# Additions of squares for the row norms on GpSimd instead of VectorE, in a two-layer hybrid encoder step

## The chip, the cores and the metric

The kernel runs on one core of a Trainium2 chip. The metric is device time in microseconds: 2740.84 us is the median of three runs of the kernel before (2739.1 to 2744.39). Engines are called as in the profile: PE (TensorE), DVE (VectorE), ACT (ScalarE), POOL (GpSimd), SP (the queue that issues most DMAs).

## The reference, cut to what matters

Two layers are computed for 1024 prompt frames and 64 frames of a running stream, 1088 columns in all, in float32. Each layer normalises its input, projects it, mixes it by gated linear attention and differential attention, projects the result (w_out), normalises that and adds it to x, then does the same with a ConvFFN.

```
def rms_norm(x, w):
    y = xf * lax.rsqrt(jnp.mean(xf * xf, axis=-1, keepdims=True) + EPS)
    return y * w
...
    h = rms_norm(x, ln_mix_pre)
    mix = concat([og, od]) @ w_out
    x = x + rms_norm(mix, ln_mix_post)
    h = rms_norm(x, ln_ffn_pre)
    ... ConvFFN ...
    x = x + rms_norm(y @ w_ffn_down, ln_ffn_post)
```

Each `rms_norm` over the 1024 features needs the mean of the squares of a row. The change touches how these squares are summed.

## The kernel before, in words

Features lie on the 128 partitions and in 8 tiles along them; the 1088 frames lie along the free dimension, in three groups (384, 384 and 320 columns, `GROUPS`). A float32 matmul is made of three passes over high and low halves of the operands (XH/XL, WH/WL, MH/ML), each with a float32r type. So every weight block costs one ACT copy (line 290, WH) and one DVE subtraction (line 269 by way of line 129, WL), and every activation that is multiplied again costs the same.

The order of each engine's instructions is written by the Python program itself, in one pass (manual schedule). `fm_block` emits a block of 24 matmuls (8 feature tiles by 3 passes) and puts off its eviction by one block. Between blocks `pump` emits steps of generators that wait in three queues: `front` (norm sums, entered with `soon` and a due time), `side` (the chains below) and `idle`. What decides is a modelled clock: `clock["pe"]` grows with every matmul and `clock["dve"]` with every call through the wrapper `V` (class `Vector`, lines 118 to 131, so that every DVE instruction carries line 129). A `front` entry is due at the greater of the PE clock plus 1.0 and the DVE clock plus 0.5; a `side` step is emitted only while the DVE clock is less than 1.5 us ahead of the PE clock. A call of `nc.gpsimd` leaves both clocks alone. Each engine then executes its own list strictly in that order.

Two stages hold the norms that the change touches.

- **Stage C** (once in each layer): w_out times the mixer output, 8 blocks a group. `ev_wo` has ACT copy each block to ACC (line 1238) and square it (line 1225 for the first, 1229 after it, into one of the two buffers `EX` in TMP). `sq_flush` (line 1218) adds that square to SQ. Then come, for the group g, `acc_norm`: `ssum` (three matmuls of 384 or 320 columns of SQ with ONE, a sum over partitions), `rstd` (ACT line 436, POOL line 437), one block later `bcast` (three matmuls with IDN, ACT copies the result to RB, line 446). After it `chain(which=1)` takes 8 steps, one for each feature tile k: ACC times RB (DVE), times a weight plus the old x in XH (DVE), square by ACT into one of the two buffers `sqb` (line 499), and the addition of the square before it to SQ (line 498, the last at 503). After the eighth, `x_norm` does `ssum`, `rstd` and `bcast` again, and eight more steps make the new XH and XL (DVE, ACT line 514, DVE). The up projection of the group waits for these.
- **Stage D** (end of each layer): the down projection, 8 blocks a group. `ev_dn` adds the block to ACC (DVE), ACT squares it, `sq_flush` adds it to SQ. In the first layer `acc_norm`, `chain(which=3)` and `x_norm` follow: each of 8 steps has three DVE operations (times RB; times weight plus XH; the XL part in `tail`), two on ACT (lines 527, 528) and one addition to SQ (line 484). In the second layer only the first sum is needed, for the outputs.

`ssum` stands in PE's list, and PE takes its list in order: as long as SQ isn't complete, all matmuls behind `ssum` wait. There are 21 such sums: six in each stage C, six in the first layer's stage D, three in the second layer's. In the texts below S means such a sum of squares, B the broadcast one block behind it; acc 0 to 2 are those of `acc_norm` for the groups 0 to 2, x 0 to 2 those of `x_norm`.

POOL's list holds before the change the `pow` of line 437, the small operations of the attention's row norm (lines 1166 to 1168, 831), and DMAs: x to the DRAM buffer XS (lines 501, 533), ConvFFN values to YD (line 1296), queries and keys to QSd and KSd (line 914).

Of the kernel before, what the change touches and what calls it, by code (L numbers as in the profile page):

```python
# [14 lines left out]
ALU = mybir.AluOpType  # L15
# [36 lines left out]
def hybrid_kernel(ctx: ExitStack, tc: tile.TileContext,  # L52
# [6 lines left out]
    nc = tc.nc  # L59
# [71 lines left out]
    V = Vector()  # L131

    def f(ap):
        return ap.bitcast(F32)
# [55 lines left out]
    def soon(gen, key, more=0.0):  # L190

        front.append([gen, max(clock["pe"] + 1.0, clock["dve"] + 0.5) + more, key])
# [185 lines left out]
    def ln(l, i, k):  # L378
        return VC[:, l, 264 + i * 8 + k:265 + i * 8 + k]
# [49 lines left out]
    def ssum(g, b):  # L429

        for j in range(3):
            t0 = tt(3 * g + j)
            mm(PS[:, b, j:j + 1], SQ[:, t0:t0 + 128], ONE, start=True, stop=True)

    def rstd(g, b, dst):
        act(dst, PS[:, b, 0:3], AF.Identity, scale=1.0 / D, bias=EPC)
        nc.gpsimd.tensor_tensor(dst, dst, NEGH[:, 0:3], ALU.pow)

    def bcast(g, b, src):

        for j in range(3):
            mm(PS[:, b, j * 128:(j + 1) * 128], src[:, j:j + 1].to_broadcast([128, 128]), IDN,
               start=True, stop=True)
        t0, n = GROUPS[g]
        if g < 2:
            act(RB[:, t0:t0 + n], PS[:, b, :n], AF.Copy)
        else:
            act(RB[:, t0:t0 + 256], PS[:, b, :256], AF.Copy)
            act(RB[:, SEQ:T], PS[:, b, 320:384], AF.Copy)
# [16 lines left out]
    def chain(l, g, which, tag):  # L466

        t0, n = GROUPS[g]
        sqb = TMP[:, 2316:3084].rearrange("p (r t) -> p r t", r=2)
        nl, nw = (l, 2) if which == 1 else (l + 1, 0)  # L470
        rb = RB[:, t0:t0 + n]
        sq = SQ[:, t0:t0 + n]
        while ("acc", g) not in done:
            yield "acc", g
        done.remove(("acc", g))

        def a(k):
            return accv[:, k, t0:t0 + n]

        def tail(k):  # L480
            V.scalar_tensor_tensor(XL[:, k, t0:t0 + n], a(k), ln(nl, nw, k),
                                   f(XH[:, k, t0:t0 + n]), ALU.mult, ALU.subtract)
            if k:
                V.tensor_tensor(sq, sq, sqb[:, k % 2, :n], ALU.add)
        def x_norm():
            ssum(g, 5)
            rstd(g, 5, RS[:, 3 * g:3 * g + 3])
            yield 1.6
            bcast(g, 6, RS[:, 3 * g:3 * g + 3])
            done.add((tag, "rs", g))  # L490
            yield

        if which == 1:
            for k in range(8):
                V.tensor_tensor(a(k), a(k), rb, ALU.mult)
                V.scalar_tensor_tensor(a(k), a(k), ln(l, which, k), f(XH[:, k, t0:t0 + n]), ALU.mult, ALU.add)
                if k > 1:
                    V.tensor_tensor(sq, sq, sqb[:, (k - 1) % 2, :n], ALU.add)
                act(sqb[:, k % 2, :n] if k else sq, a(k), AF.Square)
                if k % 4 == 3:  # L500
                    nc.gpsimd.dma_start(XS[:, k - 3:k + 1, t0:t0 + n], accv[:, k - 3:k + 1, t0:t0 + n])
                if k == 7:
                    V.tensor_tensor(sq, sq, sqb[:, 1, :n], ALU.add)
                    soon(x_norm(), (tag, "rs", g))
                yield
            while (tag, "rs", g) not in done:
                yield tag, "rs", g

            def low(k):
                x = XH[:, k, t0:t0 + n]  # L510
                V.tensor_tensor(XL[:, k, t0:t0 + n], a(k), f(x), ALU.subtract)
            for k in range(8):
                V.scalar_tensor_tensor(a(k), a(k), ln(nl, nw, k), rb, ALU.mult, ALU.mult)
                act(XH[:, k, t0:t0 + n], a(k), AF.Copy)
                if k:
                    low(k - 1)
                if k == 7:
                    low(7)
                    done.add((tag, "x", g))
                yield  # L520
            return
        V.tensor_tensor(a(0), a(0), rb, ALU.mult)
        for k in range(8):
            if k < 7:
                V.tensor_tensor(a(k + 1), a(k + 1), rb, ALU.mult)
            V.scalar_tensor_tensor(a(k), a(k), ln(l, which, k), f(XH[:, k, t0:t0 + n]), ALU.mult, ALU.add)
            act(XH[:, k, t0:t0 + n], a(k), AF.Copy, scale=ln(nl, nw, k))
            act(sqb[:, k % 2, :n] if k else sq, a(k), AF.Square)
            if k:
                tail(k - 1)  # L530
            if k == 7:
                tail(7)
                nc.gpsimd.dma_start(XS[:, :, t0:t0 + n], accv[:, :, t0:t0 + n])
                done.add((tag, "x", g))
                soon(x_norm(), (tag, "rs", g), 3.0 if which == 3 else 0.0)
            yield
# [677 lines left out]
    def sq_flush():  # L1214

        if st.get("sq"):
            sq, j = st.pop("sq")
            V.tensor_tensor(sq, sq, j, ALU.add)

    def sq_add(src, g, first):  # L1220

        t0, n = GROUPS[g]
        sq = SQ[:, t0:t0 + n]
        if first:
            act(sq, src, AF.Square)
        else:
            st["sqi"] = st.get("sqi", 0) + 1
            j = EX[:, st["sqi"] % 2, :n]
            act(j, src, AF.Square)
        sq_flush()  # L1230
        if not first:
            st["sq"] = (sq, j)

    def ev_wo(m, g, first, last):
        t0, n = GROUPS[g]

        def ev(b):
            act(accv[:, m, t0:t0 + n], PS[:, b, :n], AF.Copy)
            sq_add(PS[:, b, :n], g, first)
            if last:  # L1240
                sq_flush()
        return ev
# [263 lines left out]
    def ev_dn(first, last, m, g):  # L1506
        t0, n = GROUPS[g]

        def ev(b):
            a = accv[:, m, t0:t0 + n]  # L1510
            if first:
                act(a, PS[:, b, :n], AF.Copy)
            else:
                V.tensor_tensor(a, PS[:, b, :n], a, ALU.add)
            if last:
                sq_add(a, g, m == 0)
                if m == 7:
                    sq_flush()
                if l + 1 == DEPTH:
                    act(a, a, AF.Copy, scale=ln(l, 3, m))  # L1520
        return ev
# [59 lines left out]
    for l in range(DEPTH):  # L1581
# [168 lines left out]
        def c_blocks():  # L1750
            ring["banks"] = (0, 1, 2, 3, 4, 7)
            for g in range(3):
                residual(g)
            for n, (g, i, w) in enumerate(plan):
                m, u = L["wo"][i]
                if w:
                    want(wo[0] + w)
                fm_block(u, g, wo_rhs, ev_wo(m, g, n % 8 == 0, n % 8 == 7))
                yield
                pump(3)  # L1760
                if n % 8 == 7:
                    flush()
                    soon(acc_norm(g), ("acc", g))
                    beside(chain(l, g, 1, tag))
# [44 lines left out]
        for p in range(NP):  # L1809
            n, i = divmod(p, 7)  # L1810
# [70 lines left out]
        n = L["dn", 18]  # L1881
# [3 lines left out]
        for g in range(3):  # L1885
            ahead = range(6) if g == 0 else ()
            bs = {m: bank() for m in ahead}
            for m in ahead:
                dn_mms(bs[m], (18, 19), m, g, True, False)
                pump()  # L1890
            for m in range(8):
                if m in bs:
                    b = bs[m]
                    dn_mms(b, (20, 21), m, g, False, True)
                else:
                    b = bank()
                    dn_mms(b, (18, 19, 20, 21), m, g, True, True)
                if l + 1 < DEPTH and g == 2 and m == 6:
                    want_part(768)
                defer(lambda m=m, g=g, b=b: ev_dn(False, True, m, g)(b))  # L1900
                pump()
            if g == 2:
                want(n + 5)
            flush()
            if l + 1 < DEPTH:
                soon(acc_norm(g), ("acc", g))
                beside(chain(l, g, 3, ("D", l)))
            else:
                if g < 2:
                    soon(out_norm(g), ("acc", g))  # L1910
                else:
                    drain()
                beside(outputs(g))
# [31 lines left out]
```

## Time and profile before

| What | Value |
|---|---|
| median of 3 runs | 2740.84 us (2739.1 to 2744.39) |
| profiled execution | 2747.34 us, its span 2745.6 us |
| mean granted TensorE clock | 0.991 |
| PE busy | 2685.3 us |
| DVE busy | 1783.5 us, 3632 instructions |
| ACT busy | 1205.2 us |
| POOL busy | 271.9 us, 453 instructions |
| additions of squares on DVE | 98 of 128x384 (54.3 us) and 49 of 128x320 (23.8 us) |
| stage C of the first and the second layer | about 525 to 645 us and 1881 to 2000 us of the span |
| stage D with its norms | about 1327 to 1440 us and 2682 to 2745 us |

The profile comes from one execution. A row of a timeline gives the start, the length, engine, line, operation, output and inputs with their shapes, how many instructions were merged, and in brackets the idle time of the engine before it with what ended it. Starts of DVE operations that follow each other lie a little closer than their lengths, because they overlap by some 0.08 us.

### The profile page before, as it was taken

Reading aid. Unit: us, or ns where it says so; the run is one execution under the profiler, and the core shown is the slowest. Engines: PE = TensorE matmul, PEld = TensorE weight load, DVE = VectorE, ACT = ScalarE, POOL = GpSimd, SP = SyncE. Lnnn points to the kernel's source line nnn. Section 1 sums busy time; section 2 is a strip of 40 time slices with the busy share of each in tenths; the row PEclk is TensorE's granted clock in tenths of the full one; section 3 lists DMA queues with packets and bytes.
Section 4 is the critical chain, followed back from the end, with each engine's and each line's share of the span. In section 5 each row is a group of like instructions: output and inputs, shape, how many; then the busy total and the mean of one; then the engine's idle time right before and its main releaser. Section 6 shows DMA issues by size and latency. Waiting matters only on the chain.

```text
span 2745.6 us, 48446 instructions
## 1 busy us (share of the span) xinstructions
PE 2685.3 (98%) x19271; PEld 2626.4 (96%) x19271; DVE 1783.5 (65%) x3632; ACT 1205.2 (44%) x2484; POOL 271.9 (10%) x453
## 2 busy tenths in 40 slices
PE   8999999999999999999999999999899999999999
PEld 8999989999999999999999999889899999999998
DVE  5443458577898888445772334684788988883455
ACT  5333348555533434412343343684554333443125
POOL 2200024201000000000021000341010000000000
PEclk9999999999999999999999999999999999999999
DMA  7421176432222222323452213744331222233233
GB/s 251 142 72 51 56 194 150 127 108 80 65 87 80 71 74 94 112 85 98 136 188 86 64 42 85 206 107 134 117 95 51 78 88 71 71 108 104 73 122 124
DMA packets 296938, 284.62 MB, mean 104 GB/s; under 512 B 15438, under 2 KB 264680, under 8 KB 296712
## 3 DMA queue, kind: packets, MB, share of 16 engines
q1 hardware_dynamic: 272584, 214.14, 27.0%
q0 software_dynamic: 17344, 63.58, 6.3%
q10 hardware_dynamic: 6784, 3.81, 0.5%
q8 instruction: 152, 2.49, 0.4%
q14 instruction: 74, 0.61, 0.1%
HBM read 198.85 MB, written 82.62 MB: 103 GB/s over the span
## 4 chain that ended last, share of the span: by engine, by line
PE 85%; DVE 5%; DMA 4%; issue 3%; ACT 2%; POOL 0%; SPq 0%; ACTq 0%; DVEq 0%; POOLq 0%
PE PS L110 82%; PE PS L114 3%; DVE ACC L129 2%; DMA RAW<-in_w_out_dram 1%; DVE SML L129 1%; DMA RAW<-in_w_ffn_up_dram 1%; DVE WL L129 1%; DVE SQ L129 1%; ACT WH L290 1%; DMA out_dram<-TMP 0%; DMA WH<-QSd 0%; DVE ML L129 0%; DMA WH<-KSd 0%; ACT ACC L1112 0%; DVE XL L129 0%
## 5 line engine op out<-in xcount | busy, mean ns | idle before, releaser
L110 PE MATMUL PS<-XH,WL 128*128 128x272 f32 (+2 forms) x3600 | 664.3, 303 | 0.0
L110 PEld LDWEIGHTS PS<-XH,WL 128*128 128x128 f32 x3600 | 541.6, 189 | 0.1
L110 PE MATMUL PS<-XL,WH 128*128 128x384 f32 (+1 forms) x1680 | 399.2, 331 | 0.0
L110 PE MATMUL PS<-MH,WL 128*128 128x272 f32 (+2 forms) x1872 | 387.0, 304 | 0.0
L110 PE MATMUL PS<-XH,WH 128*128 128x384 f32 (+1 forms) x1296 | 322.0, 333 | 4.9 <-DVE TMP L129 2.7
L110 PEld LDWEIGHTS PS<-XL,WH 128*128 128x128 f32 x1680 | 299.2, 191 | 0.0
L110 PEld LDWEIGHTS PS<-MH,WL 128*128 128x128 f32 x1872 | 289.3, 189 | 0.0
L290 ACT ACTIVATE WH<-RAW 128x1024 fp32r<-128x1024 f32 (+3 forms) x177 | 147.5, 839 | 303.7 <-DMA RAW<-in_w_ffn_down_dram 180.2
L129 DVE TENSOR_TENSOR ACC<-PS,ACC 128x384 f32<-128x384 f32 (+1 forms) x264 | 139.2, 534 | 191.0 <-PE PS L110 190.8
L129 DVE TENSOR_TENSOR WL<-RAW,WH 128x1024 fp32r<-128x1024 f32 (+3 forms) x177 | 167.9, 949 | 114.8 <-ACT WH L290 114.6
L110 PEld LDWEIGHTS PS<-XH,WH 128*128 128x128 f32 x1296 | 229.1, 191 | 6.1 <-DVE TMP L129 3.6
L110 PE MATMUL PS<-XL,WL 128*128 128x272 f32 (+2 forms) x1344 | 230.6, 294 | 0.0
L110 PE MATMUL PS<-MH,WH 128*128 128x384 f32 (+1 forms) x720 | 216.5, 333 | 0.8 <-DVE XL L129 0.8
L110 PE MATMUL PS<-ML,WH 128*128 128x384 f32 (+1 forms) x720 | 214.4, 331 | 1.8 <-DVE ML L129 1.8
L1388 ACT ACTIVATE WL<-ACC 128x512 fp32r<-128x512 f32 x144 | 87.3, 629 | 253.6 <-PE PS L110 161.3
L110 PEld LDWEIGHTS PS<-XL,WL 128*128 128x128 f32 x1344 | 194.7, 188 | 0.0
L129 DVE SCALAR_TENSOR_TENSOR ACC<-ACC,VC 128x1090 f32<-128x1090 f32 x144 | 194.1, 1348 | 0.1
L110 PEld LDWEIGHTS PS<-ML,WH 128*128 128x128 f32 x720 | 134.1, 191 | 2.3 <-DVE ML L129 2.3
L110 PEld LDWEIGHTS PS<-MH,WH 128*128 128x128 f32 x720 | 131.5, 189 | 2.1 <-DVE XL L129 1.1
L129 DVE TENSOR_REDUCE SML<-PS 128x1 f32<-128x384 f32 (+6 forms) x144 | 104.4, 725 | 42.7 <-PE PS L110 41.2
L110 PE MATMUL PS<-WH,XH 128*128 128x256 f32 (+1 forms) x864 | 128.8, 292 | 0.0
L110 PE MATMUL PS<-WH,XL 128*128 128x256 f32 (+1 forms) x864 | 122.8, 285 | 0.0
(255 smaller groups left out, 4725.3 us busy)
## 6 DMA issues: line engine op xcount, KB each, us to landing
RAW<-in_w_ffn_up_dram SPq DMA_DIRECT2D x52, 512.0 KB
RAW<-in_w_in_dram SPq DMA_DIRECT2D x48, 512.0 KB
YD<-ACC POOLq DMA_DIRECT2D x36, 544.0 KB, 3.0
RAW<-in_w_out_dram SPq DMA_DIRECT2D x32, 512.0 KB
XH<-XS SPq DMA_DIRECT2D x8, 1536.0 KB
RAW<-in_w_ffn_down_dram SPq DMA_DIRECT2D x48, 256.0 KB
RB<-YD SPq DMA_DIRECT2D x22, 544.0 KB
SQ<-YD SPq DMA_DIRECT2D x18, 544.0 KB
```

The costliest lines, as they stand in the source:

```text
L110: nc.tensor.matmul(out, lhsT, rhs, **kw)
L114: nc.tensor.transpose(out, in_, idn)
L129: return op(out, *a, **kw)
L290: act(hi, src, AF.Copy)
L1388: act(hi, src, AF.Copy)
```

## The change

The additions of squares at lines 484, 498, 503 and 1218 are issued by `nc.gpsimd` instead of the wrapper `V`. Nothing else in the text changes. There are 147 of them: 84 at line 1218, 42 at 498 and 503, 21 at 484.

```
         def tail(k):
...
             if k:
-                V.tensor_tensor(sq, sq, sqb[:, k % 2, :n], ALU.add)
+                nc.gpsimd.tensor_tensor(sq, sq, sqb[:, k % 2, :n], ALU.add)
...
                 if k > 1:
-                    V.tensor_tensor(sq, sq, sqb[:, (k - 1) % 2, :n], ALU.add)
+                    nc.gpsimd.tensor_tensor(sq, sq, sqb[:, (k - 1) % 2, :n], ALU.add)
                 act(sqb[:, k % 2, :n] if k else sq, a(k), AF.Square)
...
                 if k == 7:
-                    V.tensor_tensor(sq, sq, sqb[:, 1, :n], ALU.add)
+                    nc.gpsimd.tensor_tensor(sq, sq, sqb[:, 1, :n], ALU.add)
                     soon(x_norm(), (tag, "rs", g))
...
             sq, j = st.pop("sq")
-            V.tensor_tensor(sq, sq, j, ALU.add)
+            nc.gpsimd.tensor_tensor(sq, sq, j, ALU.add)
```

Because the additions no longer advance the modelled DVE clock, the program also emits the other instructions in another order. The following piece of the difference is PE's list in stage C of the first layer, ahead of S of x 0 (the row with ONE and SQ); the six rows of a block are one weight block of 24 matmuls.

```order
 L110 MATMUL PS<-MH,WL 128x384 x4
 L110 MATMUL PS<-XL,WL 128x384 x4
-L110 MATMUL PS<-MH,WH 128x384 x4
-L110 MATMUL PS<-XL,WH 128x384 x4
-L110 MATMUL PS<-ML,WH 128x384 x4
-L110 MATMUL PS<-XL,WH 128x384 x4
-L110 MATMUL PS<-MH,WL 128x384 x4
-L110 MATMUL PS<-XL,WL 128x384 x4
 L110 MATMUL PS<-ONE,SQ 128x1 x3
```

S of x 0 stands one block earlier in PE's list. Counted in matmuls behind the B that starts the chain, S of x 0, x 1 and x 2 stood at 96, 120 and 144 before, and all three stand at 72 now, in both layers; the S of acc 1 and acc 2 stand 72 behind the B before them instead of 48 and 24. In stage D of the first layer S of x 0 stands 120 matmuls behind the B of acc 0 instead of 168, S of x 1 147 behind the B of acc 1 instead of 225, and S of x 2 129 behind the B of acc 2 instead of 230.

In the same place POOL's list held these rows before, from the first `pow` of stage C on (SML and RS hold the row scales, XS is x in DRAM).

```order
L437 TENSOR_TENSOR SML<-SML,NEGH 128x3
L501 DMA XS<-ACC 128x4x384 x2
L437 TENSOR_TENSOR RS<-RS,NEGH 128x3
L437 TENSOR_TENSOR SML<-SML,NEGH 128x3
L501 DMA XS<-ACC 128x4x384 x2
```

Now it holds these, from the first additions of stage C to the `pow` of x 0.

```order
L1218 TENSOR_TENSOR SQ<-SQ,TMP 128x384 x7
L437 TENSOR_TENSOR SML<-SML,NEGH 128x3
L498 TENSOR_TENSOR SQ<-SQ,TMP 128x384 x2
L501 DMA XS<-ACC 128x4x384
L498 TENSOR_TENSOR SQ<-SQ,TMP 128x384 x2
L1218 TENSOR_TENSOR SQ<-SQ,TMP 128x384
L498 TENSOR_TENSOR SQ<-SQ,TMP 128x384 x2
L501 DMA XS<-ACC 128x4x384
L503 TENSOR_TENSOR SQ<-SQ,TMP 128x384
L1218 TENSOR_TENSOR SQ<-SQ,TMP 128x384
L437 TENSOR_TENSOR RS<-RS,NEGH 128x3
```

Between the B of acc 0 and S of x 0 POOL has to do seven additions of the chain, one of the next group's blocks ahead of the last, and two DMA issues, all in this order.

In stage D of the first layer POOL's list ends, ahead of the `pow` of x 0, with these rows.

```order
L1218 TENSOR_TENSOR SQ<-SQ,TMP 128x384 x2
L437 TENSOR_TENSOR SML<-SML,NEGH 128x3
L484 TENSOR_TENSOR SQ<-SQ,TMP 128x384 x2
L533 DMA XS<-ACC 1024x1x384
L1218 TENSOR_TENSOR SQ<-SQ,TMP 128x320
L437 TENSOR_TENSOR RS<-RS,NEGH 128x3
```

The last two additions of the chain of group 0 now stand behind the `pow` of acc 1, and so behind S of acc 1 on PE; 14 additions stand between the two `pow` operations of acc 0 and x 0 ahead of the DMA, seven of the chain and seven of the blocks.

More of the change, by code (lines that the diff above doesn't have):

```diff
@@ L483, in tail @@
             if k:
-                V.tensor_tensor(sq, sq, sqb[:, k % 2, :n], ALU.add)
+                nc.gpsimd.tensor_tensor(sq, sq, sqb[:, k % 2, :n], ALU.add)
         def x_norm():
@@ L497, in chain @@
                 if k > 1:
-                    V.tensor_tensor(sq, sq, sqb[:, (k - 1) % 2, :n], ALU.add)
+                    nc.gpsimd.tensor_tensor(sq, sq, sqb[:, (k - 1) % 2, :n], ALU.add)
                 act(sqb[:, k % 2, :n] if k else sq, a(k), AF.Square)
@@ L502, in chain @@
                 if k == 7:
-                    V.tensor_tensor(sq, sq, sqb[:, 1, :n], ALU.add)
+                    nc.gpsimd.tensor_tensor(sq, sq, sqb[:, 1, :n], ALU.add)
                     soon(x_norm(), (tag, "rs", g))
@@ L1217, in sq_flush @@
             sq, j = st.pop("sq")
-            V.tensor_tensor(sq, sq, j, ALU.add)
+            nc.gpsimd.tensor_tensor(sq, sq, j, ALU.add)
     def sq_add(src, g, first):
```

## The prediction

> **What bounds the kernel now.** I read the page's busy times and its chain of work first.
>
> ```profile
> PE 2685.3 (98%) x19271; PEld 2626.4 (96%) x19271; DVE 1783.5 (65%) x3632; ACT 1205.2 (44%) x2484; POOL 271.9 (10%) x453
> PE 85%; DVE 5%; DMA 4%; issue 3%; ACT 2%; POOL 0%; SPq 0%; ACTq 0%; DVEq 0%; POOLq 0%
> ```
>
> PE is the bound. No addition counts as such; what counts is how long PE stands still for SQ. So the waits of PE come next: the whole run, then the windows of the two stages C (515 to 680 and 1870 to 2010 us).
>
> ```profile
> PE PS L110 <- DVE SQ L129: 15.0, 9, 3.0
> ```
> ```profile
> PE PS L110 <- DVE SQ L129: 7.3, 4, 3.0
> ```
> ```profile
> PE PS L110 <- DVE SQ L129: 7.0, 4, 2.5
> ```
>
> SQ is PE's longest wait by far: 15.0 us, of which 7.3 and 7.0 lie in the stages C and 0.7 is left for stage D. These are the prize. Where they stand in the first stage C is in PE's timeline.
>
> ```profile
> 555.75 0.83 PE L110 MATMUL PS<-IDN,SML 128*128 128x128 f32 x6
> 556.34 0.96 PE L110 MATMUL PS<-MH,WH 128*128 128x384 f32 x4
> ...
> 560.61 0.85 PE L110 MATMUL PS<-MH,WH 128*128 128x384 f32 x4
> ...
> 564.77 0.85 PE L110 MATMUL PS<-MH,WH 128*128 128x384 f32 x4
> ...
> 574.73 0.83 PE L110 MATMUL PS<-ONE,SQ 128*128 128x1 f32 x6 [1.47 <-DVE SQ L129]
> 575.42 0.94 PE L110 MATMUL PS<-MH,WH 128*128 128x384 f32 x4
> ...
> 581.24 0.83 PE L110 MATMUL PS<-IDN,RS 128*128 128x128 f32 x6
> ...
> 598.84 0.75 PE L110 MATMUL PS<-MH,WH 128*128 128x320 f32 x4
> ...
> 602.36 0.75 PE L110 MATMUL PS<-MH,WH 128*128 128x320 f32 x4
> ...
> 615.38 0.83 PE L110 MATMUL PS<-ONE,SQ 128*128 128x1 f32 x6 [2.29 <-DVE SQ L129]
> ...
> 627.65 1.15 PE L110 MATMUL PS<-ONE,SQ 128*128 128x1 f32 x6 [2.98 <-DVE SQ L129]
> 628.66 2.91 PE L110 MATMUL PS<-XH,WH 128*128 128x384 f32 x8
> ...
> 635.73 0.83 PE L110 MATMUL PS<-IDN,SML 128*128 128x128 f32 x6
> ```
>
> B of acc 0 is at 555.75; a block of 24 matmuls of 384 columns takes 4.16 us (560.61 to 564.77), of 320 columns 3.52 (598.84 to 602.36). The first block behind a B or S takes 4.27 (556.34 to 560.61). Behind the stop of 1.47 us it takes 5.82 (575.42 to 581.24), 1.6 more, and behind that of 2.98 us 7.07 (628.66 to 635.73), 2.8 more. So a stop costs 1.6 to 2.8 us of slow matmuls on top (2.2 in the mean), though not always.
>
> **What the additions cost on DVE, and what holds the chain of x 0.** ACT and DVE behind that B:
>
> ```profile
> 556.62 0.49 ACT L446 ACTIVATE RB<-PS 128x384 f32<-128x384 f32 x1 [2.97 <-PE PS L110]
> ...
> 559.51 0.52 ACT L499 ACTIVATE TMP<-ACC 128x384 f32<-128x384 f32 x1 [0.60 <-DVE ACC L129]
> ```
> ```profile
> 557.14 0.56 DVE L129 TENSOR_TENSOR ACC<-ACC,RB 128x384 f32<-128x384 f32 x1 [8.72 <-ACT RB L446]
> ...
> 558.27 0.55 DVE L129 TENSOR_TENSOR ACC<-ACC,RB 128x384 f32<-128x384 f32 x1
> ...
> 560.99 1.22 DVE L129 TENSOR_TENSOR WL<-RAW,WH 128x1024 fp32r<-128x1024 f32 x1
> 562.12 0.55 DVE L129 TENSOR_TENSOR ACC<-ACC,RB 128x384 f32<-128x384 f32 x1
> ```
> ```profile
> L129 DVE TENSOR_TENSOR SQ<-SQ,TMP 128x384 f32<-128x384 f32 x98 | 54.3, 554 | 21.7 <-ACT TMP L1229 17.7 <-ACT TMP L499 3.1
> L129 DVE TENSOR_TENSOR SQ<-SQ,TMP 128x320 f32<-128x320 f32 x49 | 23.8, 486 | 1.2 <-ACT TMP L499 0.4 <-ACT TMP L1229 0.2
> ```
>
> DVE loses 78.1 us of busy time. A step of the chain is 1.13 us without its addition (557.14 to 558.27), a WL 1.13. DVE could be through its eight steps, with the two WL among them, 8 x 1.13 + 2 x 1.13 = 11.3 us behind RB. RB is there 1.4 us behind B (555.75 to 557.11), and the first addition can begin 2.9 us behind RB (559.51 + 0.52 = 560.03).
>
> **What they cost on POOL.** The trace has no addition of this size there. What it has are small operations, grouped by tile (least, median and most ns), and one that runs into DVE.
>
> ```profile
> L1166 POOL TENSOR_SCALAR SML<-SML x72: 183/261/1093, 397.2 to 1868.4; 128x1 f32<-128x1 f32 x64, 64x1 f32<-64x1 f32 x8
> ...
> L1168 POOL TENSOR_SCALAR TMP<-TMP,SML x72: 364/372/2101, 398.5 to 1869.3; 128x128 f32<-128x128 f32 x64, 64x128 f32<-64x128 f32 x8
> ...
> L437 POOL TENSOR_TENSOR SML<-SML,NEGH x9: 848/913/1442, 552.0 to 1985.7; 128x3 f32<-128x3 f32 x9
> ```
> ```profile
> 1866.20 2.10 POOL L1168 TENSOR_SCALAR TMP<-TMP,SML 128x128 f32<-128x128 f32 x1
> ```
> ```profile
> 1865.79 2.36 DVE L129 TENSOR_TENSOR WL<-RAW,WH 128x1024 fp32r<-128x1024 f32 x2
> ```
>
> From one to 128 elements an operation with one input tensor grows from 0.18 to 0.36 us, 1.42 ns an element. With one such stream 384 columns take 0.19 + 0.55 = 0.74 us, with two of the same speed 0.19 + 1.09 = 1.28. I take the middle, 1.01 us, of which 0.82 is reading (320 columns: 0.68). [...]
>
> The last two rows matter more. L1168, 0.37 us as a rule, took 2.10 when it fell beside two DVE subtractions with both inputs in SBUF: they end at 1868.15, it ends at 1868.30. POOL could not read while DVE read two tensors. All DVE work of the chain is of that kind (ACC with RB, ACC with XH, RAW with WH). I therefore add the reading time of POOL to the DVE time, whoever of the two waits: an addition that cost DVE 0.47 us from start to start now costs the pair 0.82.
>
> **The sums S of stage C.** The change removes the additions from DVE, and the order shown with the change moves each S of an x to 72 matmuls behind its B.
>
> x 0: PE is at S 3 x 4.16 + 0.6 = 13.1 us behind B. Needed: 1.4 (RB) + 2.9 (before the first addition) + 11.3 - 2.9 = 8.4 (DVE) + 8 x 0.82 = 6.6 (seven additions of the chain, one of a block ahead of the last) = 19.3. Stop 6.2 us, where 1.47 stood.
>
> x 1: PE needs 3 x 3.52 + 0.6 = 11.2; 1.4 + 2.9 + 8.4 + 7 x 0.82 + 0.68 = 19.1. Stop 7.9, where 2.29 stood.
>
> x 2, 320 columns, beside the first blocks of the up projection:
>
> ```profile
> L129 DVE SCALAR_TENSOR_TENSOR ACC<-ACC,VC,XH 128x320 f32<-128x320 f32 x24 | 13.2, 550 | 0.6
> ...
> L129 DVE TENSOR_TENSOR ACC<-ACC,RB 128x320 f32<-128x320 f32 x24 | 11.6, 485 | 0.0
> ```
>
> A step is 0.55 + 0.49 less two overlaps of 0.05, 0.94; eight are 7.5, three weight subtractions 3.4, the convolution of two blocks with three operations of this size 3.2, seven additions 7 x 0.68 = 4.8. With RB 20.3, against 13.1. Stop 7.2, where none stood; what stood there was 144 matmuls away from its B.
>
> acc 1 and acc 2 now have 72 matmuls behind the B of the x before them instead of 48 and 24. Five additions beside the second half of the chain (8 steps of about 1.07) need up to 1.4 + 8.6 + 4.1 = 14.1 against 13.1, and 13.4 against 11.2; since the additions needn't be last, I take 1.5 together, where 0.56 (the 7.3 less the other three waits) and 2.98 stood.
>
> A stage C so stops for 6.2 + 7.9 + 7.2 + 1.5 = 22.8 us instead of 7.3 or 7.0: +31.3 for both. Slow matmuls: three long stops of 2.2 = 6.6 instead of 1.6 + 2.8 = 4.4, +4.4 for both.
>
> **Stage D of the first layer.**
>
> ```profile
> 1340.34 0.83 PE L110 MATMUL PS<-IDN,SML 128*128 128x128 f32 x6
> ```
> ```profile
> 1349.05 0.56 DVE L129 TENSOR_TENSOR ACC<-ACC,RB 128x384 f32<-128x384 f32 x1
> ...
> 1350.58 0.56 DVE L129 TENSOR_TENSOR SQ<-SQ,TMP 128x384 f32<-128x384 f32 x1
> ```
> ```profile
> 1340.00:1365.00 25.00, 21.95 (x137) 21.42 (x137) 23.08 (x48) 13.30 (x27) 1.80 (x2) 1.00 0.00 1
> 1365.00:1380.00 15.00, 12.87 (x78) 12.81 (x77) 11.70 (x25) 7.16 (x15) 1.35 (x2) 0.89 0.42 141
> ```
>
> A chain step is 1.53 us of DVE (1349.05 to 1350.58), eight 12.2. S of x 0 comes 84 matmuls of 384 and 36 of 320 columns behind B, with three S and B between: 14.6 + 5.3 + 1.8 = 21.7 us. Needed: 1.4 + 12.2 + 14 x 0.82 = 25.1: 3.4 us in S of acc 1 and x 0. x 1: 147 matmuls of 320 columns and four S and B, 24.0, against 1.4 + 12.2 + 3.4 (three weight subtractions as at 560.99) + 7 x 0.82 + 7 x 0.68 = 27.5: 3.5. x 2: 129 matmuls of 384, 24.2, against 1.4 + 8 x 1.44 (0.94 and one more operation of 0.50) + 4.8 + 3.4 = 21.1 and what the next layer's first keys and queries put between: I take 1.0, with POOL's DMAs of line 914 among its additions. With two slow stretches of 2.2 that is 12.3. Before, PE was idle for 3.05 and 2.13 us in these two windows (25.00 - 21.95, 15.00 - 12.87), and at a clock of 0.89 lost 1.65 more: 6.8. So +5.5.
>
> **The end of the second layer.**
>
> ```profile
> 2734.24 0.47 ACT L1229 ACTIVATE TMP<-ACC 128x320 f32<-128x320 f32 x1
> ```
> ```profile
> 2736.13 0.73 PE L110 MATMUL PS<-ONE,SQ 128*128 128x1 f32 x6
> ```
>
> The last square is ready 24 matmuls of transposes ahead of this S, at 2734.7; an addition of 1.01 behind it ends by 2735.8. Nothing, 0.4 us if the cover fails.
>
> **The sum.** 31.3 + 4.4 + 5.5 = +41.2 us. The profiled execution took 2747.3 us for a span of 2745.6, 6.5 us above the median of the runs; it becomes 2788.5, and the median 2740.8 + 41.2 = 2782.0, +1.5%. With streams at the fast end (0.55 of reading) each S of an x in C comes 2.2 us earlier and D is 7 us cheaper, 21 us less: 2761. At the slow end it is 21 more: 2803. A measurement of this kernel can tell about 0.2% from no change, 5.5 us.
>
> **The rivals.**
>
> *POOL waits, DVE doesn't.* Then DVE is through at 11.3 us, and each addition is only stretched as L437 was at its longest (1.44 instead of 0.87: 0.57). Up to the end of DVE's steps at 1.4 + 11.3 = 12.7 POOL gets through (12.7 - 4.3) / 1.58 = 5 additions, the other three take 3.0: 15.8, with a DMA issue 16.3. Stops of 3.2, 5.1 and about 3.5, 8 us more than before with the slow matmuls in each C, some 4 in D: 2741 + 20 = 2761. For it speaks that no DVE row of this trace is stretched; against it that POOL's operations here are too short to stretch one. [...]
>
> *No exclusion: DVE is relieved, faster.* Additions of 1.01 run beside DVE. S of x 0 is ready at 1.4 + 11.3 + 0.5 + 1.0 = 14.2 against 13.1, x 1 at 14.2 against 11.2, x 2 at 16.8 against 13.1: 7.8 us of stops, as many as before, since S has moved forward too. In D the chain needs 16.8 us with its evictions, PE is never early, and the 6.8 us go: 2734, 0.25% faster. The 2.10 us of L1168 speak against it; for it, that long rows of DVE (evictions from PSUM in D) may leave room enough.
>
> *POOL's queue is late as a whole.* The DMAs of lines 501, 1296 and 914 stand among additions that wait for ACT, ACT's squares wait for the two buffers that additions free, and ACT's weight copies and evictions stand behind those. With the slow price and 2 us for each of the nine x sums that is 2803 + 18 = 2821.
>
> That the change doesn't do what it says can be left out: POOL's list in the order holds the additions.
>
> **How the numbers follow.** Forecast (2761 to 2803) 0.55; POOL alone waits 0.15; late queue 0.10; no exclusion 0.12; a mixture that cancels, within 5.5 us of before, 0.08. So slower 0.80, same 0.08, faster 0.12. The range 2744 to 2812 takes in the forecast with both ends, the first rival, and a part of the late queue; it leaves out no exclusion and the rest of the queue, two in ten.
>
> **What would show it.** Right: PE's waits name POOL for SQ with 40 to 60 us over 12 to 15 waits, the longest 6 to 8 us at x 1 of stage C; additions on POOL have a median above 1 us with a long tail; DVE's ACC rows in the chains are longer than 0.62 us. The first rival: POOL's additions are long, DVE's rows are not. No exclusion: additions all of one length, SQ waits no larger than 15 us. It would be wrong if S of x 0 in stage C waited less than 3 us, or if PE's longest new wait were for something else than SQ.

## The result and the profile after

The changed kernel takes 2811.6 us (median of 4 runs, 2808.9 to 2818.0) where the kernel before takes 2741.0 (4 runs): a ratio of 1.0252, 95% interval 1.0234 to 1.027. It is slower by 70.6 us; 41.2 were forecast, and 2811.6 lies at the upper edge of the range, which ended at 2812, and above 2803, the slow end of the mechanism that was held most likely. The profiled execution of the changed kernel took 2811.7 us with a span of 2810.0, so its trace stands for the median; that of before had a span of 2745.6 and was 6.3 us above the median of 2741.0. The two traces therefore have to account for 64.4 us.

The page's busy times and its chain of work, as in the prediction's first fence, for the changed kernel:

```profile
PE 2700.6 (96%) x19271; PEld 2639.9 (94%) x19271; DVE 1776.6 (63%) x3485; ACT 1207.3 (43%) x2484; POOL 437.3 (16%) x600
PE 86%; DVE 7%; ACT 2%; DMA 2%; issue 2%; POOL 1%; SPq 0%; ACTq 0%; DVEq 0%; POOLq 0%
```

DVE has lost 147 instructions (3632 to 3485) and with them 78.1 us of additions, yet its busy time fell by 6.9 us only (1783.5 to 1776.6). PE has the same 19271 matmuls and is busy 15.3 us longer: its matmuls ran slower, at a mean granted clock of 0.978 against 0.991. The other 49.1 us are idle time. PE's waits (us in total, times, longest) say for what:

```profile
PE PS L110 <- POOL SQ L503: 44.0, 6, 8.8
PE PS L110 <- POOL SQ L1218: 13.4, 6, 8.9
PE PS L110 <- ACT WH L290: 8.2, 1, 8.2
PE PS L110 <- POOL SQ L484: 3.6, 1, 3.6
```

61.0 us of waits for SQ over 13 waits stand where 15.0 over 9 stood, and one of 8.2 us for a weight copy is new. PE's timeline places them. First the first stage C, where the rows with IDN are B (SML for an accumulator, RS for an x) and those with ONE are S:

```profile
557.58 0.83 PE L110 MATMUL PS<-IDN,SML 128*128 128x128 f32 x6
578.08 1.44 PE L110 MATMUL PS<-ONE,SQ 128*128 128x1 f32 x6 [7.17 <-POOL SQ L503]
...
602.86 0.83 PE L110 MATMUL PS<-IDN,SML 128*128 128x128 f32 x6
623.04 1.44 PE L110 MATMUL PS<-ONE,SQ 128*128 128x1 f32 x6 [8.79 <-POOL SQ L503]
...
643.85 0.83 PE L110 MATMUL PS<-ONE,SQ 128*128 128x1 f32 x6 [1.66 <-POOL SQ L1218]
648.81 0.83 PE L110 MATMUL PS<-IDN,SML 128*128 128x128 f32 x6
...
669.72 1.44 PE L110 MATMUL PS<-ONE,SQ 128*128 128x1 f32 x6 [5.75 <-POOL SQ L503]
```

x 0 stops 7.17 us, x 1 8.79, acc 2 1.66, x 2 5.75: 23.4 in all. The second layer's stage C is the same (7.17, 8.79, 1.68, 6.36: 24.0). Then stage D of the first layer:

```profile
1365.10 0.83 PE L110 MATMUL PS<-IDN,SML 128*128 128x128 f32 x6
...
1389.12 1.44 PE L110 MATMUL PS<-ONE,SQ 128*128 128x1 f32 x6 [8.93 <-POOL SQ L1218]
...
1414.74 2.26 PE L110 MATMUL PS<-XH,WH 128*128 128x384 f32 x6 [8.24 <-ACT WH L290]
...
1453.74 1.44 PE L110 MATMUL PS<-ONE,SQ 128*128 128x1 f32 x6 [3.59 <-POOL SQ L484]
```

Windows around the three places show where the 64.4 us lie. The columns are the window, its length, and then busy time and instructions of PE, PEld, DVE, ACT and POOL, PE's granted clock, and DMA. Before (first layer's stage C, stage D, second layer's stage C):

```profile
520.00:670.00 150.00, 142.66 (x844) 141.15 (x844) 96.82 (x182) 74.25 (x147) 12.36 (x15) 0.97 0.36 110
1330.00:1445.00 115.00, 107.49 (x654) 106.44 (x653) 84.63 (x170) 54.49 (x113) 21.18 (x26) 0.97 0.46 148
1870.00:2030.00 160.00, 150.96 (x891) 149.11 (x891) 101.97 (x195) 77.73 (x154) 13.00 (x16) 0.97 0.36 112
```

After:

```profile
520.00:685.00 165.00, 140.34 (x801) 138.06 (x801) 96.44 (x135) 73.11 (x144) 62.22 (x56) 0.91 0.34 103
1330.00:1470.00 140.00, 118.39 (x693) 116.65 (x692) 95.76 (x138) 56.43 (x111) 60.33 (x60) 0.91 0.42 137
1910.00:2080.00 170.00, 142.87 (x817) 140.32 (x817) 97.87 (x139) 74.53 (x147) 62.91 (x56) 0.91 0.34 103
```

PE's idle time (length less busy) grew from 7.34 to 24.66 us in the first stage C, from 9.04 to 27.13 in the second, from 7.51 to 21.61 in stage D: 17.3 + 18.1 + 14.1 = 49.5. The three stages so hold all of the new idle time (49.1 us in the whole run); with the 15.3 us by which PE's busy time grew in the whole run it is 64.8, against 64.4 from the spans.

What the additions did to DVE is seen in its groups of rows (busy time in us, mean ns of one). After:

```profile
L129 DVE TENSOR_TENSOR WL<-RAW,WH 128x1024 fp32r<-128x1024 f32 x91 | 126.1, 1390 | 70.3 <-ACT WH L290 70.0
L129 DVE TENSOR_TENSOR ACC<-PS,ACC 128x384 f32<-128x384 f32 x176 | 96.6, 555 | 140.1 <-PE PS L110 140.1
L129 DVE TENSOR_TENSOR ACC<-ACC,RB 128x384 f32<-128x384 f32 x48 | 40.5, 848 | 57.4 <-ACT RB L446 57.4
```

Before, the same groups:

```profile
L129 DVE TENSOR_TENSOR WL<-RAW,WH 128x1024 fp32r<-128x1024 f32 x91 | 110.9, 1220 | 68.9 <-ACT WH L290 68.7
L129 DVE TENSOR_TENSOR ACC<-PS,ACC 128x384 f32<-128x384 f32 x176 | 96.8, 555 | 132.1 <-PE PS L110 132.1
L129 DVE TENSOR_TENSOR ACC<-ACC,RB 128x384 f32<-128x384 f32 x48 | 26.4, 554 | 27.0 <-ACT RB L446 27.0
```

Operations with both inputs in SBUF grew: ACC with RB from 554 to 848 ns, RAW with WH from 1220 to 1390. The same tensor_tensor with one input in PSUM (ACC with PS) stayed at 555, and the 13 of these that run beside an addition in the first layer's stage D took 0.54 to 0.56 us (384 columns) and 0.48 (320). On the other side POOL's additions, by tile (least, median and most ns):

```profile
L1218 POOL TENSOR_TENSOR SQ<-SQ,TMP x84: 738/1010/1872, 530.4 to 2799.0; 128x384 f32<-128x384 f32 x56, 128x320 f32<-128x320 f32 x28
L498 POOL TENSOR_TENSOR SQ<-SQ,TMP x36: 861/1213/1973, 561.9 to 2060.4; 128x384 f32<-128x384 f32 x24, 128x320 f32<-128x320 f32 x12
```

The medians are above 1 us with a tail to 2, where the least for 384 columns is 0.86: both engines are stretched.

### The profile page after: what moved, and what is told of

It is laid out like the page before. It is cut to its first block, busy times and chain, and to the rows that moved or that the text cites. A ratio compares the mean times of both kernels' runs of the same rounds, so it can differ in the third digit from the quotient of the medians.

```text
span 2810.0 us, 48556 instructions
## 1 busy us (share of the span) xinstructions
PE 2700.6 (96%) x19271; PEld 2639.9 (94%) x19271; DVE 1776.6 (63%) x3485; ACT 1207.3 (43%) x2484; POOL 437.3 (16%) x600
## 4 chain that ended last, share of the span: by engine, by line
PE 86%; DVE 7%; ACT 2%; DMA 2%; issue 2%; POOL 1%; SPq 0%; DVEq 0%; ACTq 0%; POOLq 0%
PE PS L110 83%; DVE ACC L129 4%; PE PS L114 3%; DVE WL L129 1%; DMA RAW<-in_w_out_dram 1%; DVE SML L129 1%; DVE XL L129 1%; DVE ML L129 0%; ACT WH L290 0%; DVE TMP L129 0%; DMA WH<-KSd 0%; DMA out_dram<-TMP 0%; POOL SQ L498 0%; ACT ACC L1112 0%; POOL SQ L503 0%
## 5 line engine op out<-in xcount | busy, mean ns | idle before, releaser
L129 DVE TENSOR_TENSOR WL<-RAW,WH 128x1024 fp32r<-128x1024 f32 (+3 forms) x177 | 183.1, 1036 | 116.4 <-ACT WH L290 116.1
L1218 POOL TENSOR_TENSOR SQ<-SQ,TMP 128x384 f32<-128x384 f32 (+1 forms) x84 | 90.1, 1072 | 570.0 <-ACT TMP L1229 569.1
L1481 POOL DMA_DIRECT2D YD<-ACC x36 | 19.2, 533 | 744.5 <-DVE ACC L129 710.4
```

The source lines that it names most:

```text
L129: return op(out, *a, **kw)
L1218: nc.gpsimd.tensor_tensor(sq, sq, j, ALU.add)
L1481: nc.gpsimd.dma_start(YD[NC + n], y[:, :T])
```

## The experiments

The change does two things: another engine does the additions, and, since a call to GpSimd does not advance the modelled DVE clock, the program is emitted in another order. The theory was that both cost, and that the additions cost on GpSimd because it and DVE exclude each other in reading SBUF. The rivals were that the order alone does it, that GpSimd's latency alone does it, and that DVE is relieved where S isn't moved. In the diffs below `tick` advances the modelled clock as the wrapper of VectorE does.

**The order alone.** At the four lines:

```diff
-V.tensor_tensor(sq, sq, j, ALU.add)
+nc.vector.tensor_tensor(sq, sq, j, ALU.add)
```

> All additions on VectorE as before, but the modelled clock is not advanced for them, so that TensorE's list is that of the changed kernel (S of each x in stage C 72 matmuls behind its B). Theory: the pair of VectorE and GpSimd is no faster than VectorE alone, and what costs time is mostly that S has moved forward. Before, S of x 0 was ready 19.0 us and S of x 1 20.7 us behind B (574.73 - 555.75, 615.38 - 594.65), in the changed kernel 20.5 and 20.2. So here S waits about 5.9 us at x 0 and 8 at x 1, SQ waits are 30 to 45 us in all, and the time is 2770 to 2795. Rival, that GpSimd's additions are what costs and the order is harmless: SQ waits stay near 15 us and the time within 10 us of 2741.

Measured: 2789.1 us, ratio 1.0158 (1.0135 to 1.018). S of x 0 is ready 16.8 us behind its B (558.34 to 575.14) and stops 3.46; x 1 16.7 and 5.34. SQ waits are 38.7 us, 12.3 of them for additions of line 1218, the longest 6.2 in stage D, and the weight copy there waits 5.9. So with the additions still on VectorE the new order costs 43 us, within the range of the theory, and the new stops of stage D come from it too. The single stops were smaller than expected because S became ready sooner as well: fewer instructions stand ahead of it in DVE's list (one WL and one addition fewer at x 0, two of each at x 1). From this run to the changed kernel the lists of PE, ACT and DVE are the same but for the additions; there S of x 0 and x 1 moves from 16.8 and 16.7 to 20.5 and 20.2 us behind B. That is what the engine alone does in the new order.

**The engine alone.** The same lines, in the order of before (the lists of PE, ACT and DVE are row for row those of the kernel before, but for the additions):

```diff
-V.tensor_tensor(sq, sq, j, ALU.add)
+tick(j.shape[1]); nc.gpsimd.tensor_tensor(sq, sq, j, ALU.add)
```

> All 147 additions on GpSimd, but the modelled clock is advanced for each as VectorE's wrapper does, so that TensorE's list is that of the kernel before. Theory: S of x 0 stands 96 matmuls behind B (17.5 us) and is ready after 20.5: a stop of 3.0; x 1 17.9 to 18.4 against 20.2: about 2; x 2 none; acc 1 and acc 2 3 to 6 together; 8 to 11 us a stage C instead of 7, some 5 more in stage D: 2745 to 2762. Rival, that GpSimd's price and late queue are the cost wherever S stands: 2785 or more. Rival, that VectorE is relieved once S is not moved forward: 2735 or less.

Measured: 2786.0 us, ratio 1.0146 (1.0121 to 1.017). The theory's range was missed, and the first rival's number was met. S of x 0 stops 4.77 us and x 1 5.58, in the second layer 4.75 and 5.89; S is ready 22.27 and 24.27 us behind B where VectorE alone needs 18.98 and 20.73. The expectation had carried over 20.5 from the changed kernel, whose list has less ahead of S. With the order fixed, GpSimd makes each of these S 3.3 and 3.5 us later. Most of that is DVE and not GpSimd's own delay: DVE's last chain operation ends 3.0 us later behind B at x 0 and 3.2 at x 1. The two effects, 43 and 40 us, don't add up to the 70.6 of both: the SQ waits do (23.7 and 20.7 us more, and 46.0 with both), PE's longer busy time doesn't (15.9, 14.6, and 15.3 with both).

**Parts of the engine's effect.** In the order of before, only the chains' additions (lines 484, 498, 503) on GpSimd, and only those of line 1218.

> Only the 63 additions of the chains (lines 484, 498, 503) on GpSimd, those of line 1218 on VectorE, TensorE's list that of the kernel before. Theory: the chain's own additions are hidden neither from VectorE nor from S: x 0 and x 1 stop 2 to 3 us each as with all of them, acc 1 and acc 2 as before: 2741 to 2755. Rival, relief: 2735 or less.

> Only the 84 additions of line 1218 on GpSimd, those of the chains on VectorE, TensorE's list that of the kernel before. Theory: they fall beside VectorE operations with two SBUF inputs too and cost the pair 0.82 us instead of 0.47; with 4 to 5 of them inside each chain, S of x comes 1 to 2 us later: 2741 to 2752. Rival, that they run beside VectorE freely: VectorE is relieved of 5 x 0.47 = 2.4 us in each chain, the stops of 1.47 and 2.29 us vanish: 2728 to 2737.

Measured: 2773.6 us, ratio 1.0099 (1.0077 to 1.012), and 2765.3, ratio 1.0069 (1.0042 to 1.0095). Both miss the theory's numbers upward and the rivals' by far: neither part is free. In the first, S of x 0 is ready 21.9 us behind B, in the second 20.7, where 18.98 stood. Besides the stops, both lose in slower matmuls, which the expectations had left out: the granted clock of the profiled execution is 0.984 and 0.989 against 0.991 (in the second it was the fastest of four, the others have 0.985 and 0.986).

Over the whole kernel the two parts differ. DVE's busy time is 1783.5 us before, 1804.1 with the 63 additions of the chains on GpSimd and 1761.3 with the 84 of line 1218: the first load DVE although it has fewer instructions, the second relieve it, though not where a chain needs it.

**Does GpSimd hold VectorE, and by what?** Two runs in the order of before, with all lists but GpSimd's identical to those of the run with the engine alone. In the first each addition is a write of ones (0.41 us at the least for 384 columns), in the second a copy with one input (0.51 in the chains of x 0 and x 1); the sums of squares are left out in both.

```diff
-tick(j.shape[1]); nc.gpsimd.tensor_tensor(sq, sq, j, ALU.add)
+tick(j.shape[1]); nc.gpsimd.memset(j, 1.0)
```
```diff
-tick(j.shape[1]); nc.gpsimd.tensor_tensor(sq, sq, j, ALU.add)
+tick(j.shape[1]); nc.gpsimd.tensor_copy(sq, j)
```

> The run with all additions on GpSimd in the order of before, with each addition replaced by a GpSimd write of ones over the buffer that holds the square; the sums of squares are left out, so S waits for squares alone. What the run is for is VectorE's time between its first operation with RB and its last with XH in the chain of x 0 and x 1 of the first stage C: 15.8 and 17.6 us before, with 9 and 10 additions among them, 18.7 and 20.7 with the additions on GpSimd. Theory, that GpSimd's reading is what holds VectorE: 11.5 and 13 us here, no VectorE row with ACC and RB over 0.6 us, and the time 2715 to 2735. Rival, that any work on GpSimd holds VectorE: 14 us or more, and stretched rows.

> The same, with each addition replaced by a GpSimd copy of the square's buffer into SQ: one input tensor instead of two; the sums are left out. Theory, that an operation that reads at all holds VectorE, and for the time that it reads (one stream, about 0.55 us instead of 0.8): VectorE's time in the chains of x 0 and x 1 is 16 to 17.5 and 18 to 19.5 us, and the time 2755 to 2775, between the run with the additions and the kernel before. Rival, that only operations with two inputs hold VectorE: 11.5 and 13 us as without reading, 2715 to 2735.

Measured: 2720.0 us, ratio 0.9915 (0.9893 to 0.9937), with writes; 2734.9, ratio 0.9965 (0.9952 to 0.9977), with copies. DVE's first and last rows of the chain of x 0, up to the last with XH, in the run with the engine alone:

```profile
557.74 0.56 DVE L129 TENSOR_TENSOR ACC<-ACC,RB 128x384 f32<-128x384 f32 x1 [17.72 <-ACT RB L446]
...
561.12 2.04 DVE L129 TENSOR_TENSOR WL<-RAW,WH 128x1024 fp32r<-128x1024 f32 x1
563.08 1.37 DVE L129 TENSOR_TENSOR ACC<-ACC,RB 128x384 f32<-128x384 f32 x1
...
568.95 2.03 DVE L129 TENSOR_TENSOR WL<-RAW,WH 128x1024 fp32r<-128x1024 f32 x1
570.90 1.37 DVE L129 TENSOR_TENSOR ACC<-ACC,RB 128x384 f32<-128x384 f32 x1
...
575.85 0.62 DVE L129 SCALAR_TENSOR_TENSOR ACC<-ACC,VC,XH 128x384 f32<-128x384 f32 x1
```

And POOL in the same stretch:

```profile
568.57 1.33 POOL L1218 TENSOR_TENSOR SQ<-SQ,TMP 128x384 f32<-128x384 f32 x1
569.86 2.00 POOL L498 TENSOR_TENSOR SQ<-SQ,TMP 128x384 f32<-128x384 f32 x1
```

These rows run in turns. The addition of 568.57 ends at 569.90; the WL that began beside it at 568.95 ends 1.08 us after that, at 570.98. The addition that began at 569.86 ends 0.88 us after the WL, at 571.86, and the ACC with RB that began at 570.90 ends 0.41 us after the addition, at 572.27. Once the other is through, each takes about its undisturbed time (1.22, 0.86 and 0.55): 0.14 us less, 0.02 more and 0.14 less, so in these rows neither makes more than 0.14 us of headway while it is held.

In the run with writes:

```profile
555.12 0.56 DVE L129 TENSOR_TENSOR ACC<-ACC,RB 128x384 f32<-128x384 f32 x1 [17.75 <-ACT RB L446]
...
558.49 1.22 DVE L129 TENSOR_TENSOR WL<-RAW,WH 128x1024 fp32r<-128x1024 f32 x1
559.63 0.55 DVE L129 TENSOR_TENSOR ACC<-ACC,RB 128x384 f32<-128x384 f32 x1
...
566.97 0.62 DVE L129 SCALAR_TENSOR_TENSOR ACC<-ACC,VC,XH 128x384 f32<-128x384 f32 x1
```

DVE does the same work, 16 operations of the chain and three WL, in 12.47 us (555.12 to 567.59) beside writes and in 18.73 (557.74 to 576.47) beside additions. Eight GpSimd operations start within it, so one addition takes 6.26 / 8 = 0.78 us from DVE, where the addition on DVE itself took 0.47 (15.76 us before with seven of them; the expectation says nine). Beside copies it is 14.96 us, 0.31 for each. At x 1 the same stretch took 17.02 us beside writes, not the 13 expected: 3.2 of them DVE waited for weight copies (ACT line 290), so its own work took 13.8. It is 20.72 beside nine additions, 0.77 for each. The groups of ACC with RB say the same for the whole kernel. Copies:

```profile
L129 DVE TENSOR_TENSOR ACC<-ACC,RB 128x384 f32<-128x384 f32 x48 | 31.6, 663 | 48.3 <-ACT RB L446 48.3
```

Writes:

```profile
L129 DVE TENSOR_TENSOR ACC<-ACC,RB 128x384 f32<-128x384 f32 x48 | 26.3, 552 | 48.0 <-ACT RB L446 48.0
```

So reading is what holds DVE here: beside copies its rows grew to 663 ns, and beside operations of GpSimd that only write they stayed at 552, against 554 before. A write is not much shorter than a copy (0.41 and 0.51 us), so the length alone is not what counts. DVE's busy time was 1716.6 us beside writes, 1737.7 beside copies, 1775.7 beside additions, for one and the same list. Over the whole kernel an addition on GpSimd so takes (1775.7 - 1716.6) / 147 = 0.40 us from DVE and on DVE (1783.5 - 1716.6) / 147 = 0.46. Split by number, the runs with parts give an estimate of 0.78 us for an addition of the chains and 0.19 for one of line 1218. Of the chains' 63 additions 58 overlap a DVE operation with two SBUF inputs in the run with the engine alone, of the 84 of line 1218 only 38. The rival that only operations with two inputs hold DVE falls, since copies stretch it too; the theory's number for the copies (16 us or more, 2755 us) was too high. Three groups of rows sum it up: with both inputs in SBUF, ACC with RB went from 554 to 848 ns beside additions and to 552 beside writes; with one input in PSUM, ACC with PS stayed at 555 with the additions on GpSimd.

**S later.** The stops could be given back by asking for S later. With GpSimd, in the order of before as the starting point, and with VectorE, the kernel before with two settings:

```diff
-soon(x_norm(), (tag, "rs", g))
+soon(x_norm(), (tag, "rs", g), 8.0)
-soon(acc_norm(g), ("acc", g))
+soon(acc_norm(g), ("acc", g), 3.0)
```

The first run on VectorE has 2.0 and 3.0 in these places for all groups, the second only for x 0 and acc 2.

> All additions on GpSimd with the clock advanced, and S in stage C asked for later: 8 us of the model for each x, 3 for each accumulator. S of x 0 then stands 144 matmuls behind B (25 us of TensorE), x 1 192 (28 us), x 2 144. Theory: S is ready 22.3 and 24.3 us behind B as in the run with the order of before, so the long stops of the x go, some 27 us with what follows them of slow matmuls come back, what remains is acc 1, acc 2 and stage D: 2745 to 2765, no faster than the kernel before. Rival, that VectorE's longer chain is late at other places as soon as S no longer waits (the XH of the up projection, weight subtractions): 2775 or more. Rival, that the additions on GpSimd are worth something once S is late enough: 2735 or less.

> The kernel before, additions on VectorE, with S in stage C asked for later alone: 2 us of the model for each x, 3 for each accumulator, which puts the S of x 0 120 matmuls behind B instead of 96, of x 1 168 instead of 120 and of x 2 168 instead of 144. Theory, that the stops for SQ were the prize and not VectorE's load: x 0 and x 1 no longer stop, acc 2 stops 1 to 2 us, 8 to 16 us less with the slow matmuls: 2725 to 2735. Rival, that a later S makes the split of x late for the up projection: 2741 or more.

> The kernel before, additions on VectorE, with S in stage C later only where it stopped: x 0 (120 matmuls behind its B instead of 96) and acc 2 (192 behind the B of x 1 instead of 168); x 2 keeps its distance from the start of the up projection (120 behind its B instead of 144). Theory: S was ready 19.0, 20.7 and about 33 us behind these B, TensorE now comes 21.5, 21.5 and 32 to 33 us behind them, so no stop is left at x 0 and x 1 and less than 1 us at acc 2; x 2 stops 0 to 2 us; the up projection finds XH ready because x 2 is no later than before. 5 to 12 us less than before: 2730 to 2738. Rival: VectorE and ScalarE are late for XH as with all S later (8.7 us there): 2741 or more.

Measured: on GpSimd 2791.6 us, ratio 1.0172 (1.015 to 1.0193); on VectorE 2742.2, ratio 0.9994 (0.9978 to 1.0009), and 2741.7, ratio 0.9993 (0.9979 to 1.0007). PE's waits on GpSimd:

```profile
PE PS L110 <- ACT XH L514: 15.5, 28, 1.8
PE PS L110 <- POOL SQ L503: 7.8, 2, 3.9
PE PS L114 <- DVE TMP L129: 6.4, 2, 3.4
PE PS L110 <- POOL SML L437: 5.9, 3, 2.7
```

On VectorE, with all S of stage C later:

```profile
PE PS L110 <- ACT XH L514: 8.7, 16, 1.7
PE PS L110 <- DMA WH<-KSd: 4.7, 2, 2.5
```

Most stops for SQ go, on VectorE all of those in stage C, and PE waits for XH of the up projection instead: the rival with that mechanism was right in both. On GpSimd PE was also busy 9.5 us longer than with the engine alone (2709.4 and 2699.9). With only x 0 and acc 2 later, the rival's time came (2741 or more) but not by its mechanism: S of x 1 still stops 2.33 us, since it is now ready 24.3 us behind its B (591.62 to 615.90) instead of 20.7, and the SQ waits are 11.1 us in all. A reading that fits all three, and that no run tests by itself, is that DVE has too much to do in stage C, and that a stop at S is only the place where it shows. No run with the sums in it beat the kernel before.

**Stage D.** The changed kernel with S of acc 1 in stage D 120 matmuls behind its B instead of 84:

```diff
-soon(acc_norm(g), ("acc", g))
+soon(acc_norm(g), ("acc", g), 4.0 * (g == 1))
```

> The changed kernel, with the S of acc 1 in stage D of the first layer 120 matmuls behind its B instead of 84, 6.2 us of TensorE later. If its stop of 8.9 us comes from its place alone, 6 us of it go and the wait of 8.2 us for the weight copy WH stays as it is: 2800 to 2806. If VectorE and ScalarE are the bound of that stretch, the stop moves on to the weight copy, which then waits 10 us or more, and the time is 2807 to 2815.

Measured: 2805.1 us, ratio 1.022 to the kernel before (1.0199 to 1.024), where the change has 1.0252 (1.0234 to 1.027): 6.5 us less by the medians, with intervals that overlap a little. S of acc 1 is ready 24.05 us behind the B ahead of it, as in the change (24.02), so its stop falls with its place alone, from 8.93 to 3.68 us. The weight copy's wait fell too, from 8.24 to 4.60, but a wait of 4.0 for the `pow` of an x (line 437) came up. So a part of the stop moved on, though not to the weight copy; neither of the two expectations holds whole, though the time is in the first one's range.

## Why the prediction was right, and where it was too small

**The mechanism.** POOL and DVE hold each other, DVE waits too (ACC with RB 848 ns instead of 554), and an addition of a chain costs the pair more than it cost DVE (0.78 us instead of 0.47 in the chain of x 0). The forecast took 0.82 us for a pair of engines, from the half-way price between one and two input streams; 0.78 was measured. The mutual hold was not shown by the trace of before, whose only row was the 2.10 us of line 1168, and DVE's half of it is shown now. The signs named for it came, the sizes a little over what was named: 61.0 us of SQ waits (40 to 60) over 13 waits, additions with a median above 1 us, ACC rows of 0.85 us; the longest wait is 8.9 us instead of 6 to 8, and it lies in stage D, not at x 1 of stage C (8.79). That the price of 0.82 was so near is partly luck: an undisturbed addition, taken at 1.01 us, is about 0.86 (the least of 384 columns at line 1218), and nearly all of it counts, not four fifths of a longer one. It is also luck that the time is within the range, by 0.4 us: the range had been widened beyond 2803 for another mechanism, the late queue.

**The sums of stage C.** Needed were 19.3, 19.1 and 20.3 us behind B for x 0, x 1 and x 2; measured are 20.50 (557.58 to 578.08), 20.18 (602.86 to 623.04) and 20.91 (648.81 to 669.72). At x 0 a DMA issue of 0.77 us (line 501), which the sum had left out, stands between POOL's last two additions of the chain. The stops of a stage were forecast at 22.8 us and are 23.4 and 24.0; the single ones at 6.2, 7.9, 7.2 and 1.5, and are 7.17, 8.79, 5.75 (6.36) and 1.66 (1.68). PE's idle time of both stages grew by 35.4 us for a forecast of 31.3.

**Stage D was mis-sized.** The step "3.4 us in S of acc 1 and x 0" failed. It compared PE's arrival at S of x 0, 21.7 us behind B, with the need of the whole chain. But S of acc 1 comes first, 84 matmuls (24.02 less the stop of 8.93: 15.1 us) behind B, and the additions of acc 1 stand in POOL's list between those of the chain: its last was through 24.0 us behind B. So 8.93 us stood there, and none at x 0. The weight copy of 8.24 us was in no term; it was the rival of the late queue that said weight copies would stand behind. The copy (line 290, 1413.38 on ACT) stood in ACT's list behind lines 527 and 528, which waited for DVE's ACC; ACT waited for POOL to free a buffer for 3.8 us only. In place of 2.7 us of new idle time stage D has 14.1. The run with the order alone has 6.22 and 5.93 us at these two places, so most of this term comes from the order.

**The slow matmuls were mis-sized.** The step "a stop costs 1.6 to 2.8 us of slow matmuls" failed too, as it took the short stops of before for the long ones. The term "2.2 us of slow matmuls" for a long stop, with 2.75 for stage D, made 7.2 us; PE's busy time grew by 15.3. The block behind the stop of 7.17 us:

```profile
579.38 1.63 PE L110 MATMUL PS<-MH,WH 128*128 128x384 f32 x4
580.81 1.48 PE L110 MATMUL PS<-XL,WH 128*128 128x384 f32 x4
582.09 1.48 PE L110 MATMUL PS<-ML,WH 128*128 128x384 f32 x4
583.37 1.48 PE L110 MATMUL PS<-XL,WH 128*128 128x384 f32 x4
584.65 0.95 PE L110 MATMUL PS<-MH,WL 128*128 128x384 f32 x4
```

Four matmuls take 1.28 us from start to start (580.81 to 582.09) instead of 0.69 (4.16 us for 24 in the block of 560.61 before), up to 584.65; the granted clock is 0.50 there. From S to the next B it is 8.06 us (578.08 to 586.14), where 4.84 stood without a stop (552.74 to 557.58): 3.2 us more, and 2.9 and 3.4 behind the stops of x 1 and x 2. In the run without any wait of a sum for SQ (the writes) PE was busy 2668.7 us, at a granted clock of 1.00. Measured from there the kernel before pays 16.6 us for slow matmuls, the changed one 31.9.

**The sum.** Too small by 4.1 us in the stops of stage C, 11.4 in those of stage D, 8.1 in slow matmuls; 41.2 + 23.6 = 64.8, and the spans differ by 64.4. The rest up to 70.6 is that the profiled execution of before was above its median.

**The rivals.** POOL alone waits: it falls with DVE's rows (848 ns). No exclusion: it falls by the same rows; the run that has none, with writes in place of additions, takes 2720, but it also leaves the sums out, so it doesn't show what the rival's kernel would take. The late queue: right that weight copies come late in stage D, but by way of DVE, for which ACT waits; ACT's waits for buffers that additions free are 3.8 us.

## What to carry to other kernels

Before work is moved from VectorE to GpSimd, price the pair by what VectorE does at that moment: beside VectorE operations with two SBUF inputs an addition here cost VectorE 0.78 us, nearly its whole undisturbed time on GpSimd (0.86), against 0.47 on VectorE itself, and a copy 0.31; elsewhere it cost less (0.19 by the estimate for line 1218). Neither VectorE's instruction count (147 fewer) nor its whole busy time (6.9 us less) told it; the mean time of its rows, before and after, did (554 and 848 ns). Where an order is planned from a model of one engine's time, work that leaves the model moves everything else as well; here the order cost 43 us by itself and 31 on top of the engine's 40, so run the order and the engine apart. A stop at one semaphore can be the sign of an engine that is late for others too: with S later PE waited for XH instead (15.5 us on GpSimd; 8.7 on VectorE, where the time came to 0.9994 of that before).

## What the runs showed of the hardware that was not expected

A GpSimd copy of 384 columns with one input took 0.51 us at the least in the chains of x 0 and x 1, some six tenths of an addition's 0.86, and held DVE 0.31 us against 0.78; the expectation had taken 0.55 for the time that it holds DVE.

Slow matmuls came behind a stop of only 1.47 us, and not at once. In the kernel before, behind this stop and the six short matmuls of S, four matmuls from 576.21 on still take 0.76 us from start to start, near 0.69, and the next eight 0.32 each:

```profile
576.21 0.97 PE L110 MATMUL PS<-XL,WH 128*128 128x384 f32 x4
576.97 1.48 PE L110 MATMUL PS<-ML,WH 128*128 128x384 f32 x4
578.25 1.48 PE L110 MATMUL PS<-XL,WH 128*128 128x384 f32 x4
579.53 1.18 PE L110 MATMUL PS<-MH,WL 128*128 128x384 f32 x4
```

The granted clock is 0.50 from 577.0 to 580.0, and 0.80 and 0.79 in the half microseconds on both sides: some 3.4 us in all. Around the stop of 7.17 us it is 0.50 from 575.0, within the stop, to 584.5, so that 6.6 us of it fall on matmuls. But behind the stop of 2.29 us in the same stage of the kernel before it stays at 1.00 (613.0 to 623.0), and from S to the next B it is 4.29 us (615.38 to 619.67). So the length of a stop alone doesn't decide; what does, no run here shows.
